# Turning attention weights by one transfer of strided squares, and tile 5 with them

## The chip, the cores and the metric

The kernel runs on one core of one Trainium2 chip. The core has five engines with queues of their own: TensorE (PE; its weight loads are shown apart as PEld), VectorE (DVE), ScalarE (ACT), GpSimd (POOL) and SyncE (SP), which in this kernel issues every transfer. The metric is the device time in microseconds. Profiled times are of one execution.

## The reference, cut to what matters

One layer of a hybrid encoder, for a prompt of 1024 positions and a sample of 32. Model width 1024; eight heads of A and eight of B, 64 wide each.

```python
def band_attention(q, k, v, q_pos, k_pos, bias_table):          # A
    s = jnp.einsum('bqhd,bkhd->bhqk', q, k).astype(jnp.float32) * ATTN_SCALE
    s = s + bias_table[:, rel].astype(jnp.float32)[None]
    s = jnp.where(ok[None, None], s, NEG_INF)                   # own chunk of 64 and the 8 before
    w = jax.nn.softmax(s, axis=-1).astype(v.dtype)
    return jnp.einsum('bhqk,bkhd->bqhd', w, v)

def stick_breaking(q, k, v, q_pos, k_pos):                      # B
    z = jnp.einsum('bqhd,bkhd->bhqk', q, k).astype(jnp.float32) * ATTN_SCALE
    causal = (k_pos[None, :] < q_pos[:, None])[None, None]
    log_1m = jnp.where(causal, jax.nn.log_sigmoid(-z), 0.0)
    after = lax.cumsum(log_1m, axis=3, reverse=True) - log_1m
    w = jnp.where(causal, jnp.exp(jax.nn.log_sigmoid(z) + after), 0.0).astype(v.dtype)
    return jnp.einsum('bhqk,bkhd->bqhd', w, v)
```

Before them stands an input projection of the normalised rows to q, k, v and a gate for A and for B; after them the gated output projection, a norm, and a second gate. Keys and values are outputs too. All is in float32.

## The kernel before

**Stages.** The rows are normalised and turned (0 to about 45 us), then the eight pairs of heads are worked off in the order A0, B0, A1, B1, A2, B2, A3, B3. While the attention of one pair runs, the q, k and v projections of the next pair are woven in as dense work for TensorE (`weave`, from L1311); beside the last pair the gate projections take their place. The output and gate products come at the end, from about 600 us.

**Precision.** A float32 product is made of two or three passes over operands split into a rounded high part and the rest. A tile that TensorE is to read is therefore written twice, by a cast on ScalarE to the high part and by a subtraction on VectorE for the low part (in attention: `wTh` and `wTl`).

**One head.** `attention` (from L834) works on the 1024 queries as eight query tiles of 128. `scores(i)` makes tile i: TensorE the products S in PSUM; in A VectorE adds the bias and finds the minimum and ScalarE takes the exponential; in B ScalarE takes the sigmoid, VectorE runs a scan and GpSimd subtracts neighbours. The weights then stand in `w1` (ring `be`), with queries on the partitions; `w0` (ring `om`) holds what came before. Tile i has `cost(i)` blocks of 128 keys: 1, 2, 3, 4, 5, 5, 5, 5 in A, and 1 to 8 in B.

`weights_t(i)` turns the weights, so that keys stand on the partitions, and has two ways:

- By TensorE: one transpose for each block into PSUM (`ptw`), four blocks to a bank, and from each bank a cast and a subtraction.
- By a round trip, for the tiles named in `ROUND` (4 and 6 before the change). VectorE transposes the 32 x 32 squares of `w1` into `w0`; SyncE writes `w0` to DRAM (`swap`); four transfers, one for each quarter of 32 partitions, bring the squares back into `w1`; then one cast and one subtraction over all columns.

`values(g)` is the product with v for tiles 0 to 3 (g = 0) and 4 to 7 (g = 1), and needs all their turned weights.

**The values' own round trip.** `values_out` (from L728) turns the projected v of a pair (128 x 1024) in the same way, with `vx` as the tile in between and back into `st`.

**Order.** The program is recorded first, and the planner (`plan`, L418, and `due`, L393) then simulates the engines with a cost for each operation (`cost`, L340) and lays down one fixed order for each of them. TensorE prefers attention to dense work. Tiles are turned two units after their scores (`LAG_T`, L32), so tile 5 is turned after the scores of tile 7. The rings `om` and `be` (L559) hand out room in turn: a new tile waits until the users of what lay there are done. A transfer waits at the head of SyncE's queue, and what is behind it waits too.

Of the kernel before, what the change touches and what calls it, by code (L numbers as in the profile page):

```python
# [13 lines left out]
P = 128  # L14
D = 1024
SEQ = 1024
# [11 lines left out]

ROUND = {"A": ((4,),(6,)), "B": ((4,),(6,))}
LAG_T = 2  # L32
LAG_V = 2
SPACE_S = 0.1
# [8 lines left out]
def f(ap):  # L43

    return ap.bitcast(F32)
# [454 lines left out]
def stream_step(  # L500
# [7 lines left out]
    nc = rec  # L508
    dma = nc.sync.dma_start
# [7 lines left out]
    def psum(tag, name):  # L517
        return ps.tile([P, 512], F32, tag=tag, name=name, bufs=PS_BUFS[tag])

    def scratch(shape, name):  # L520
        return Buf(shape, F32, name=name, real=dram.tile(shape, F32, tag=name, name=name))
# [3 lines left out]
    og_dr = scratch([8, P, T], "og_dr")  # L525
    h1_dr = scratch([T, D], "h1_dr")
    sum_dr = {w: scratch([4, 4, P, 512], f"sum_dr{w}") for w in "og"}
    r_dr = scratch([8, 768], "r_dr")
    vs_dr = {ab: scratch([NS, 512], f"vs_dr{ab}") for ab in "AB"}
    ple_dr = scratch([T, D], "ple_dr")  # L530

# [83 lines left out]
    def load_x(t):  # L615
        n = min(P, T - t * P)
        if t == 3:
            x34.append(at.tile([P, ringh.cols], F32, tag="wTh", name="x34")[:, 0:2 * D].rearrange("p (a c) -> p a c", a=2))
        xt = x34[0][:, t - 3] if t in (3, 4) else ring0.tile([P, D], f"x{t}")
        dma(xt[0:n], x_prompt[0, t * P:t * P + n, :] if t < 8 else x_sample[0])  # L620
# [8 lines left out]
    def scale_x(t, xt, n, gp):  # L629
        sq = ring1.tile([P, D], f"sq{t}")  # L630
        ms = small.tile([P, 1], F32, tag="ms", name=f"ms{t}", bufs=4)
        nc.scalar.activation(sq[0:n], xt[0:n], AF.Square, scale=1.0 / 32.0, accum_out=ms[0:n])
        r = rstd_of(ms, f"rs{t}", n)
        for kh in range(2):
            nc.vector.scalar_tensor_tensor(sq[0:n, HALF[kh]], xt[0:n, HALF[kh]], r[0:n], gp[kh][0:n], ALU.mult, ALU.mult)
        return sq
# [68 lines left out]
    def short_block(src, out, nm):  # L705
        pt = psum("T", nm)
        nc.tensor.transpose(pt[0:NS, 0:P], src[:, SEQ:T], ident)
        nc.scalar.copy(out[0:NS, 8, :], pt[0:NS, 0:P])
# [19 lines left out]
    def values_out(ab, p, src, o_p, o_s, then):  # L728

        h2 = slice(2 * p, 2 * p + 2)  # L730
        b0 = 4 if ab == "A" else 0
        box = {}

        def turn():
            st = src()
            D = scratch([P, SEQ], f"swap{ab}{p}")
            x = at2.tile([P, SEQ], F32, tag="tok", name=f"vx{ab}{p}", bufs=2)
            nc.vector.transpose(x.rearrange("p (c b f) -> p b c f", c=4, f=32), st[:, 0:SEQ])
            dma(D, x)
            for c in range(4):  # L740
                part = D[:, c * 256:(c + 1) * 256].rearrange("(g t) x -> t g x", t=32)
                dma(st[32 * c:32 * c + 32, 0:SEQ].rearrange("t (g x) -> t g x", g=4), part)
            out = at2.tile([P, NT, P], F32, tag="tok", name=f"vt{ab}{p}", bufs=2)
            box["out"] = out
            short_block(st, out, f"ptv{ab}{p}")

        def back():
            out = box["out"]
            nc.scalar.copy(out[:, 0:8, :].rearrange("p b (g f) -> p g b f", g=4), src()[:, 0:SEQ].rearrange("p (g b f) -> p g b f", g=4, f=32))
            dma(o_p[0, 0, :, h2, :].rearrange("(b p) h d -> p b (h d)", p=P), out[:, b0:8, :])  # L750
            dma(o_s[0, 0, :, h2, :].rearrange("p h d -> p (h d)"), out[0:NS, 8, :])
            then(out)

        return [(0.1, turn), (0.0, back)]
# [79 lines left out]
    def attention(ab, p, h):  # L834

        nm = f"{ab}{p}{h}"
# [12 lines left out]
        def lo_block(i):  # L849
            return max(0, i - 4) if ab == "A" else 0  # L850

        together = {i: g for g in ROUND[ab] for i in g}
        whole, done_with = {}, []

        def cost(i):
            return i + 1 - lo_block(i)
# [63 lines left out]
        def weights_t(i):  # L920
            g = i // 4
            step, size = LAID[ab, g]
            if g not in wT:
                wT[g] = [x.tile([P, size * P], f"{x.name}{nm}_{g}") for x in (ringh, ringl)]
            b0 = lo_block(i)
            w0, w1 = state.pop(i)
            n = i + 1 - b0
            at_ = ((i - 4 * g) * step + b0) * P
            hi, lo = (x[:, at_:at_ + n * P] for x in wT[g])
            if i in together:  # L930

                group = together[i]
                done_with.append((i, hi, lo))
                if i != group[-1]:
                    return
                w0, w1 = whole[group]
                m = sum(cost(x) for x in group)
                first = {x: sum(cost(y) for y in group[:k]) for k, x in enumerate(group)}
                squares = w0[:, 0:m * P].rearrange("p (c b q) -> p b c q", c=4, q=32)
                for x, _, _ in done_with:  # L940
                    y = slice(first[x], first[x] + cost(x))
                    nc.vector.transpose(squares[:, y], w1[:, y.start * P:y.stop * P])
                dr = scratch([P, m * P], f"swap{nm}_{i}")
                dma(dr, w0[:, 0:m * P])
                for c in range(4):
                    x = dr[:, c * m * 32:(c + 1) * m * 32].rearrange("(g k) x -> k g x", k=32)
                    dma(w1[32 * c:32 * c + 32].rearrange("k (g x) -> k g x", g=4), x)
                turned = w1.rearrange("p (g b q) -> p g b q", g=4, q=32)
                for x, hi, lo in done_with:
                    src = turned[:, :, first[x]:first[x] + cost(x), :]  # L950
                    hi, lo = (y.rearrange("p (b g q) -> p g b q", g=4, q=32) for y in (hi, lo))
                    nc.scalar.copy(hi, src)
                    nc.vector.tensor_tensor(lo, src, f(hi), ALU.subtract)
                done_with.clear()
                return
            for b in range(0, n, 4):
                m = min(4, n - b)
                pt = psum("T", f"ptw{nm}_{i}_{b}")
                for x in range(m):
                    nc.tensor.transpose(pt[:, x * P:(x + 1) * P], w1[:, (b + x) * P:(b + x + 1) * P], ident)  # L960
                c = slice(b * P, (b + m) * P)
                nc.scalar.copy(hi[:, c], pt[:, 0:m * P])
                nc.vector.tensor_tensor(lo[:, c], pt[:, 0:m * P], f(hi[:, c]), ALU.subtract)
# [26 lines left out]
        for i in range(8):  # L990
            out["S", i] = (0.107 * cost(i) + SPACE_S, lambda i=i: scores(i))
            out["T", i] = (0.107 * cost(i) + SPACE_T, lambda i=i: weights_t(i))
# [255 lines left out]
    for n in range(-1, 8):  # L1248
        a = len(order)
        if n < 7:  # L1250
            ab, p = pairs[n + 1]
# [458 lines left out]
    def short_product(nm, left, q):  # L1710
        o1, o2, both, minus = left
        acc = psum("S", f"{nm}8_{q}")[0:2 * NS]
        todo = ((o1, "B11"), (o2, "B21")) if q == 0 else ((both, "B22"), (minus, "T3"))
        i = 0
        for a, key in todo:
            for kt in range(KT):
                for part in range(2):
                    nc.tensor.matmul(acc, a[:, kt, :], blocks[nm, key][:, part, kt, :], start=(i == 0), stop=(i == 4 * KT - 1))
                    i += 1
        y = at2.tile([P, 512], F32, tag="bias", name=f"{nm}j8_{q}", bufs=2)  # L1720
        nc.scalar.copy(y[0:NS], acc[NS:2 * NS])
        nc.vector.tensor_tensor(y[0:NS], acc[0:NS], y[0:NS], ALU.add)
        return y[0:NS]
# [31 lines left out]
    for m, (nm, src, group) in enumerate(sets):  # L1755
        last_set = m == len(sets) - 1
        state = [{}, {}]
        for n, prod in enumerate(ORDER):
            for pair, t in enumerate(group):
                st = state[pair]  # L1760
# [28 lines left out]
                b = blocks[nm, WHICH[prod]]  # L1789
# [70 lines left out]
        if m in (0, 2):  # L1860
            if m == 0:
                row = Row(8, fb.tile([P, D], F32, tag="GP", name="h1_8"))
                row.load()
                for q in range(2):
                    y = short_product(nm, short, q)
# [3 lines left out]
            else:  # L1869
                for q in range(2):  # L1870
                    g8 = Gate(8, HALF[q])
                    y = short_product(nm, short, q)
# [38 lines left out]
```

## Time and profile before

| what | value |
|---|---|
| median of 3 runs | 799.42 us (797.0, 802.35, 799.42) |
| the profiled execution | 796.26 us |
| its span, first to last instruction | 794.2 us |
| granted TensorE clock, mean | 0.999 |

The page also shows in 40 slices of the span (19.9 us each) how busy the engines are, in tenths, and the DMA engines' mean busy share:

```profile
PE   9999989999999999999999999999999999999997
PEld 7999989999999999999999999999997877888786
DVE  6716868887688889877878788883354878676655
ACT  5636765767686548874677586532348967875741
POOL 5624546874547675424670436787544358597613
...
DMA  8519987668887759744544776756489847668634
```

A 9 is 90% or more. A matmul's end is modelled and overlaps the next one's start, so a busy share of PE says that it has work, not that it runs at its peak. A line with `xN | busy, mean ns | idle` is a group of N instructions: the time in which at least one of them ran, the mean of one, and how long the engine stood idle just before them, with what ended that. All instructions carry the line of one helper, L494, so they are told apart by their tiles.

### The profile page before, as it was taken

Reading aid. Unit: us, or ns where it says so; the run is one execution under the profiler, and the core shown is the slowest. Engines: PE = TensorE matmul, PEld = TensorE weight load, DVE = VectorE, ACT = ScalarE, POOL = GpSimd, SP = SyncE. Lnnn points to the kernel's source line nnn. Section 1 sums busy time; section 2 is a strip of 40 time slices with the busy share of each in tenths; the row PEclk is TensorE's granted clock in tenths of the full one; section 3 lists DMA queues with packets and bytes.
Section 4 is the critical chain, followed back from the end, with each engine's and each line's share of the span. In section 5 each row is a group of like instructions: output and inputs, shape, how many; then the busy total and the mean of one; then the engine's idle time right before and its main releaser. Section 6 shows DMA issues by size and latency. Waiting matters only on the chain.

```text
span 794.2 us, 14262 instructions
## 1 busy us (share of the span) xinstructions
PE 781.9 (98%) x4646; PEld 723.1 (91%) x4646; DVE 572.6 (72%) x1007; ACT 503.8 (63%) x1061; POOL 438.9 (55%) x503
## 2 busy tenths in 40 slices
PE   9999989999999999999999999999999999999997
PEld 7999989999999999999999999999997877888786
DVE  6716868887688889877878788883354878676655
ACT  5636765767686548874677586532348967875741
POOL 5624546874547675424670436787544358597613
PEclk9999999999999999999999999999999999999999
DMA  8519987668887759744544776756489847668634
GB/s 264 170 42 289 229 246 206 180 183 234 233 256 225 206 164 280 194 135 159 132 118 148 169 208 189 234 177 190 126 269 332 282 138 267 225 222 301 232 126 133
DMA packets 160971, 161.08 MB, mean 203 GB/s; under 512 B 39153, under 2 KB 120793, under 8 KB 160898
## 3 DMA queue, kind: packets, MB, share of 16 engines
q1 hardware_dynamic: 160898, 160.18, 67.4%
q8 instruction: 37, 0.61, 0.3%
q14 instruction: 36, 0.29, 0.1%
HBM read 99.23 MB, written 52.49 MB: 191 GB/s over the span
## 4 chain that ended last, share of the span: by engine, by line
PE 91%; DMA 2%; DVE 2%; POOL 2%; issue 1%; ACT 1%; SPq 1%; DVEq 0%; ACTq 0%; POOLq 0%
PE mm_gB L494 6%; PE mm_gA L494 6%; PE mm_qB L494 6%; PE mm_kB L494 6%; PE mm_vA L494 5%; PE mm_kA L494 5%; PE mm_vB L494 5%; PE mm_qA L494 5%; PE PVB L494 4%; PE SB L494 4%; PE SA L494 4%; PE PVA L494 4%; PE ptwB L494 3%; PE g0P L494 2%; PE g1P L494 2%; PE o1P L494 2%
## 5 line engine op out<-in xcount | busy, mean ns | idle before, releaser
L494 POOL TENSOR_TENSOR be<-om 128x384 f32<-128x384 f32 (+7 forms) x64 | 79.0, 1241 | 64.7 <-DVE om L494 38.8
L494 DVE TENSOR_TENSOR_SCAN om<-om,SB 128x384 f32<-128x384 f32 (+5 forms) x96 | 94.2, 999 | 8.7 <-ACT om L494 7.6
L494 ACT ACTIVATE om<-SB 128x384 f32<-128x384 f32 (+5 forms) x96 | 44.4, 492 | 34.0 <-DVE SB L494 23.0
L494 ACT ACTIVATE be<-om,statA 128x640 f32<-128x640 f32 (+4 forms) x64 | 44.5, 696 | 10.1 <-DVE statA L494 6.5
L494 ACT CAST wTh<-ptwB 128x512 fp32r<-128x512 f32 (+3 forms) x64 | 29.4, 481 | 19.5 <-PE ptwB L494 12.2
L494 DVE TENSOR_TENSOR wTl<-ptwB,wTh 128x512 fp32r<-128x512 f32 (+3 forms) x64 | 34.0, 547 | 10.4 <-ACT wTh L494 7.4
L494 DVE TENSOR_TENSOR wTl<-be,wTh 128x640 fp32r<-128x640 f32 (+1 forms) x32 | 35.3, 1105 | 4.7 <-ACT wTh L494 4.3
L494 DVE TENSOR_TENSOR wTl<-ptwA,wTh 128x512 fp32r<-128x512 f32 (+2 forms) x64 | 30.3, 483 | 10.3 <-ACT wTh L494 9.0
L494 DVE CUSTOM_DVE_ANT_0 om<-SA,biasA 128x320 f32<-128x320 f32 (+2 forms) x64 | 29.7, 483 | 9.0 <-PE SA L494 8.3
L494 ACT CAST wTh<-ptwA 128x512 fp32r<-128x512 f32 (+2 forms) x64 | 26.1, 424 | 13.3 <-PE ptwA L494 11.5
L494 DVE STREAM_TRANSPOSE om<-be 128x640 f32<-128x640 f32 (+1 forms) x32 | 29.0, 906 | 6.1 <-POOL be L494 3.5
L494 PE MATMUL SB<-klB,LB 128*128 128x384 f32 (+5 forms) x96 | 33.0, 348 | 0.0
L494 PE MATMUL SB<-kdB,LB 128*128 128x384 f32 (+5 forms) x96 | 32.9, 347 | 0.1
L494 POOL TENSOR_TENSOR oB<-oB,oB 128x256 f32<-128x256 f32 x32 | 24.2, 777 | 13.8 <-DMA oB<-in_w_out_dram 12.5
L494 DVE TENSOR_TENSOR SB<-SB,maskb 128x128 f32<-128x128 f32 x64 | 17.7, 292 | 19.1 <-PE SB L494 19.0
L494 PE MATMUL SA<-klA,LA 128*128 128x320 f32 (+2 forms) x96 | 29.4, 319 | 1.1 <-DMA klA<-klA 1.1
L494 PE MATMUL SA<-kdA,LA 128*128 128x320 f32 (+2 forms) x96 | 30.0, 323 | 0.0
L494 POOL TENSOR_TENSOR gB<-gB,gB 128x256 f32<-128x256 f32 x32 | 26.0, 832 | 6.8 <-DMA gB<-in_w_ple_gate_dram 6.7
L494 PE MATMUL ptwA<-ident,be 128*128 128x128 f32 x160 | 26.2, 273 | 2.7 <-ACT sumrowA L494 2.7
L494 ACT CAST wTh<-be 128x640 fp32r<-128x640 f32 (+1 forms) x32 | 25.0, 781 | 6.1 <-DMA be<-swapA 4.1
L494 PE MATMUL ptwB<-ident,be 128*128 128x128 f32 x192 | 28.7, 273 | 0.0
L494 POOL TENSOR_TENSOR sggA<-sggA,oggA 128x352 f32<-128x352 f32 x24 | 24.9, 1038 | 5.2 <-DMA be<-swapB 2.9
(707 smaller groups left out, 2655.0 us busy)
## 6 DMA issues: line engine op xcount, KB each, us to landing
swapA<-om SPq DMA_DIRECT2D x16, 320.0 KB, 3.6
be<-swapA SPq DMA_DIRECT2D x64, 80.0 KB, 2.8
oB<-in_w_out_dram SPq DMA_DIRECT2D x16, 256.0 KB
sum_dro<-oB SPq DMA_DIRECT2D x16, 256.0 KB, 4.3
gB<-in_w_ple_gate_dram SPq DMA_DIRECT2D x16, 256.0 KB, 4.2
sum_drg<-gB SPq DMA_DIRECT2D x16, 256.0 KB, 2.6
x<-in_x_prompt_dram SPq DMA_DIRECT2D x16, 256.0 KB, 4.1
h_dr<-h SPq DMA_DIRECT2D x8, 512.0 KB, 4.2
```

The costliest lines, as they stand in the source:

```text
L494: getattr(getattr(tc.nc, o.what[0]), o.what[1])(*args, **kw)
```

## The change

Tile 5 joins tiles 4 and 6 of every head on the round trip, as a group of its own. And the round trip's layout is another, for the weights and for the values: before, a VectorE transpose took 32 neighbouring columns for a square; now it takes every fourth column of a block of 128. The DRAM buffer gets a leading dimension of 4 (the quarter of partitions that the queries came from), and the key that row belongs to can be written as one running index, so a single transfer over all 128 partitions brings the squares back in place of four over 32. The write stays one transfer with one unbroken run for each partition, and the runs that are read back keep their length.

```diff
-ROUND = {"A": ((4,),(6,)), "B": ((4,),(6,))}
+ROUND = {"A": ((4,),(5,),(6,)), "B": ((4,),(5,),(6,))}
...
         def turn():
             st = src()
-            D = scratch([P, SEQ], f"swap{ab}{p}")
+            D = scratch([4, P, SEQ // 4], f"swap{ab}{p}")
             x = at2.tile([P, SEQ], F32, tag="tok", name=f"vx{ab}{p}", bufs=2)
-            nc.vector.transpose(x.rearrange("p (c b f) -> p b c f", c=4, f=32), st[:, 0:SEQ])
-            dma(D, x)
-            for c in range(4):
-                part = D[:, c * 256:(c + 1) * 256].rearrange("(g t) x -> t g x", t=32)
-                dma(st[32 * c:32 * c + 32, 0:SEQ].rearrange("t (g x) -> t g x", g=4), part)
+            nc.vector.transpose(x.rearrange("p (c b f) -> p b c f", c=4, f=32), st[:, 0:SEQ].rearrange("p (b t c) -> p b c t", c=4, t=32))
+            dma(D.rearrange("g (t c) x -> (g t) (c x)", c=4), x)
+            dma(st[:, 0:SEQ].rearrange("p (g x) -> p g x", g=4), D.rearrange("g p x -> p g x"))
...
                 for x, _, _ in done_with:
                     y = slice(first[x], first[x] + cost(x))
-                    nc.vector.transpose(squares[:, y], w1[:, y.start * P:y.stop * P])
-                dr = scratch([P, m * P], f"swap{nm}_{i}")
-                dma(dr, w0[:, 0:m * P])
-                for c in range(4):
-                    x = dr[:, c * m * 32:(c + 1) * m * 32].rearrange("(g k) x -> k g x", k=32)
-                    dma(w1[32 * c:32 * c + 32].rearrange("k (g x) -> k g x", g=4), x)
+                    nc.vector.transpose(squares[:, y], w1[:, y.start * P:y.stop * P].rearrange("p (b k c) -> p b c k", c=4, k=32))
+                dr = scratch([4, P, m * 32], f"swap{nm}_{i}")
+                dma(dr.rearrange("g (k c) x -> (g k) (c x)", c=4), w0[:, 0:m * P])
+                dma(w1.rearrange("p (g x) -> p g x", g=4), dr.rearrange("g p x -> p g x"))
```

Counted over the kernel: 88 PE transposes go (5 for each of 8 heads of A, 6 for each of 8 of B), 16 VectorE transposes and 16 round trips come, and a round trip is two transfers in place of five.

## The prediction

> **What bounds the kernel now.** I read the page first (the engines' busy shares, the chain that ended last, the DMA share), then TensorE's own waits.
>
> ```profile
> span 794.2 us, 14262 instructions
> ...
> PE 781.9 (98%) x4646; PEld 723.1 (91%) x4646; DVE 572.6 (72%) x1007; ACT 503.8 (63%) x1061; POOL 438.9 (55%) x503
> ...
> q1 hardware_dynamic: 160898, 160.18, 67.4%
> ...
> PE 91%; DMA 2%; DVE 2%; POOL 2%; issue 1%; ACT 1%; SPq 1%; DVEq 0%; ACTq 0%; POOLq 0%
> ```
>
> TensorE (PE) is busy for 98% of the span and makes 91% of the chain that ended last. Work taken from PE shortens the kernel, as long as nothing new makes PE wait. In TensorE's list of waits, those inside the attention stage are few:
>
> ```profile
> PE ptwA L494 <- ACT sumrowA L494: 2.7, 1, 2.7
> ...
> PE SA L494 <- DMA klA<-klA: 1.1, 1, 1.1
> ```
>
> Together they are 3.8 us. The dense projections fill PE whenever attention is not ready. The change touches attention alone, which runs from about 66 to 570 us. I cut it into the eight head pairs, A and B by turns, by the times at which their last outputs leave. The columns after the length are the busy us of PE, of its weight loads, of VectorE (DVE), ScalarE and GpSimd, each with its instruction count; then the granted clock, the DMA share and GB/s.
>
> ```profile
> 66.00:112.00 46.00, 42.18 (x278) 40.63 (x276) 33.88 (x80) 33.05 (x73) 20.38 (x26) 1.00 0.95 273
> 112.00:180.00 68.00, 67.92 (x430) 65.64 (x429) 56.47 (x85) 43.17 (x88) 48.13 (x54) 1.00 0.67 192
> 180.00:240.00 60.00, 60.00 (x397) 58.18 (x397) 43.17 (x104) 45.38 (x100) 28.76 (x44) 1.00 0.83 234
> 240.00:308.00 68.00, 67.37 (x436) 64.85 (x436) 58.76 (x94) 40.95 (x92) 51.67 (x61) 1.00 0.73 218
> 308.00:346.00 38.00, 38.00 (x250) 36.64 (x249) 30.27 (x72) 31.04 (x71) 13.70 (x18) 1.00 0.82 218
> 346.00:418.00 72.00, 72.00 (x460) 70.11 (x459) 58.75 (x92) 46.11 (x93) 38.60 (x39) 1.00 0.44 124
> 418.00:472.00 54.00, 54.00 (x363) 52.57 (x363) 41.85 (x101) 39.94 (x93) 14.10 (x22) 1.00 0.66 176
> 472.00:570.00 98.00, 98.00 (x626) 96.00 (x624) 67.89 (x102) 44.18 (x96) 67.54 (x70) 1.00 0.63 189
> sum 504.00, PE 499.47 PEld 484.62 DVE 391.05 ACT 323.81 POOL 282.88; mean PE 62.43 PEld 60.58 DVE 48.88 ACT 40.48 POOL 35.36
> ```
>
> PE fills every pair but the first. VectorE comes second: 391 of 504 us, 78%, and in the second B pair 58.76 of 68, or 86%. The granted clock is 1.00 throughout, so it isn't a term. DMA is nearly full in the first A pair alone (0.95).
>
> **What leaves TensorE.** Tile 5 of a head has 5 key blocks in A and 6 in B, one PE transpose each, for 8 heads of each kind: 88 of the 160 + 192. The 273 ns of one overlap its neighbours, so I take what a run of transposes costs from the timeline, as the time from its start to the start of what follows.
>
> ```profile
> L494 PE MATMUL ptwB<-ident,be 128*128 128x128 f32 x192 | 28.7, 273 | 0.0
> L494 PE MATMUL ptwA<-ident,be 128*128 128x128 f32 x160 | 26.2, 273 | 2.7 <-ACT sumrowA L494 2.7
> ```
> ```profile
> 75.27 0.71 PE L494 MATMUL ptwA<-ident,be 128*128 128x128 f32 x5
> 75.73 0.57 PE L494 MATMUL mm_kB<-hnl,wh_kB 128*128 128x352 f32 x2
> ...
> 163.18 0.82 PE L494 MATMUL ptwB<-ident,be 128*128 128x128 f32 x6
> 163.75 0.57 PE L494 MATMUL mm_qA<-hnl,wh_qA 128*128 128x352 f32 x2
> ```
>
> Five cost 0.46 us and six 0.57 us. So 8 x 0.46 + 8 x 0.57 = 8.2 us leave PE, all on the path.
>
> **What VectorE and ScalarE get.** The groups by shape:
>
> ```profile
> L494 DVE TENSOR_TENSOR_SCAN om<-om,SB 128x512 f32<-128x512 f32 x24 | 30.3, 1262 | 0.8 <-ACT om L494 0.5 <-POOL ksS L494 0.2
> L494 DVE TENSOR_TENSOR wTl<-be,wTh 128x640 fp32r<-128x640 f32 x24 | 24.3, 1012 | 4.5 <-ACT wTh L494 4.1
> L494 DVE TENSOR_TENSOR_SCAN om<-om,SB 128x384 f32<-128x384 f32 x24 | 23.9, 994 | 1.3 <-ACT om L494 1.2
> L494 DVE TENSOR_TENSOR wTl<-ptwB,wTh 128x512 fp32r<-128x512 f32 x32 | 21.5, 679 | 7.4 <-ACT wTh L494 4.7 <-PE PVB L494 2.6
> L494 DVE STREAM_TRANSPOSE om<-be 128x640 f32<-128x640 f32 x24 | 20.1, 839 | 6.1 <-POOL be L494 3.5 <-ACT be L494 2.2
> L494 DVE TENSOR_TENSOR wTl<-ptwA,wTh 128x512 fp32r<-128x512 f32 x24 | 16.5, 688 | 6.9 <-ACT wTh L494 6.6
> L494 DVE TENSOR_TENSOR wTl<-be,wTh 128x896 fp32r<-128x896 f32 x8 | 11.1, 1383 | 0.2 <-ACT wTh L494 0.2
> L494 DVE STREAM_TRANSPOSE om<-be 128x896 f32<-128x896 f32 x8 | 8.8, 1105 | 0.1
> L494 DVE TENSOR_TENSOR wTl<-ptwB,wTh 128x256 fp32r<-128x256 f32 x16 | 6.6, 413 | 1.1 <-ACT wTh L494 1.1
> L494 DVE TENSOR_TENSOR wTl<-ptwA,wTh 128x128 fp32r<-128x128 f32 x24 | 6.6, 280 | 1.3 <-ACT wTh L494 1.3
> L494 DVE STREAM_TRANSPOSE ktA<-stkA 128x512 f32<-128x512 f32 x4 | 2.8, 703 | 11.4 <-ACT stkA L494 11.4
> ```
>
> An A head gives up two evictions from PSUM (688 + 280 ns) and gets a 640 transpose (839) and a 640 subtraction in SBUF (1012): 0.88 us more. A B head gives up 679 + 413 and gets 768 columns of each; between the rows for 640 and 896 that is about 972 + 1198: 1.08 us more. Eight of each make 15.7 us on VectorE. At 391 of 504 us it has room for this beside PE, so it costs nothing; what it costs without that room is a rival below. ScalarE casts the same columns from another place, two calls becoming one, and is at 324 of 504: nothing.
>
> All 56 transposes then also read every fourth column. No row shows a strided read. The transposes for 512, 640 and 896 columns lie on one line of 1.05 ns a column, though the first writes densely and the others in runs of 32. The slowest VectorE op by the column is the scan, (1262 - 994) / 128 = 2.1 ns. So the stride costs between 0 and 1.05 ns a column; a gain I exclude, since a broken-up write pattern already changes nothing. The columns are 8 x 1920 in A, 8 x 2304 in B and 8 x 1024 for the values, 41,984 in all: 0 to 44 us of VectorE time. I take the low end, since the nearest rows are transposes of the same operation at one pace whatever the pattern; the high end is the first rival.
>
> **What the queue and the transfers get.** Quoted: the issues of the returns and of a weight load (min, median and max ns); then, around TensorE's longest attention wait, SyncE's queue in the timeline and two pieces of the chain.
>
> ```profile
> L494 SPq DMA_DIRECT2D be<-swapA x64: 302/432/866, 84.0 to 467.6; - x64
> ...
> L494 SPq DMA_DIRECT2D wr_kA<-in_w_in_dram x8: 383/612/1670, 6.9 to 310.1; - x8
> ```
> ```profile
> 108.06 3.93 SPq L494 DMA_DIRECT2D be<-swapA  x8
> ```
> ```profile
> 104.41 2.85 DMA swapA<-om
> ...
> 111.56 2.61 DMA be<-swapA
> ```
>
> A round trip's four returns take about 4 x 432 = 1728 ns to issue. One return of 512 runs (128 partitions, 4 each) is nearest to the weight loads, also 128 x 4: 612 ns. So the 40 existing round trips each give back 1.1 us of the queue, 45 us in all, and the 16 new ones take 16 x (432 + 612), about 17 us. From 108.06 us on, the issue of eight returns, 3.93 us, lies on the chain between the landing of the write and that of the returns, so some shortening is possible; the bound is the 3.8 us of waits above. I take none.
>
> Each new trip also adds a wait: SyncE's queue stands until the write has landed (2.85 us in the chain) before it can issue the return, and behind it stand weight loads and attention outputs. That is how the 2.7 us wait came about: the output's transfer was issued behind that landing, ScalarE's sum row waited for it, and PE for the row. Of the 40 trips now, one did this; 16 more at that rate cost 16/40 x 2.7 = 1.1 us. The values of tile 5 themselves aren't urgent: tile 7 is worked off after them, ahead of the product.
>
> The new trips move 8 x 2 x 320 KB and 8 x 2 x 384 KB (128 partitions of 640 or 768 columns of 4 bytes, out and back), 11.5 MB. At 67.4% of 794 us for 160 MB that is 3.3 us a MB, 38 us of DMA time over 504 us, 7 points. Only the first pair is short of room: 1.3 MB, 4.4 us, bring its 0.95 over 1 by some 2 us. Bounds 0 and 2 us; I take 1.0.
>
> **The sum.** -8.2 + 1.1 + 1.0 = -6.1 us. The profiled execution took 796.26 us (span 794.2), so it would take 790.2; it is 3.2 us below the median of the runs shown, 799.42. On that median I forecast 793. Alone, this case reaches from 787 (all of -8.2 and the 3.8 us of waits gone) to 798 (the new waits three times as dear).
>
> **Rivals.** *The strided read runs at half pace and VectorE becomes the bound.* For it: VectorE has little room in the B pairs. An A pair gets 2 x (0.88 + 2.0) + 1.07 = 6.8 us, a B pair 2 x (1.08 + 2.4) + 1.07 = 8.0. The second B pair would have 66.8 of 68 us, the third A pair 37.1 of 38. If VectorE can't run denser than the 86.4% it has shown, six of the eight pairs stretch, by 1.1, 6.7, 0, 9.3, 4.9, 5.3, 2.3 and 0 us: 29.6 us. If it can run at 100%, none does. Half of it, 14.8, gives 799.4 - 6.1 + 14.8 = 808; the ends are 793 and 823. It decides from 6.1 us of stretch on. Against it: equal pace of the transposes so far.
>
> [...]
>
> *The queue's new waits eat the gain.* If 3 of the 16 new trips, not 16/40 of one, stall PE for 2.7 us as the one above, 8.1 us are gone: 799. For it: the queue is in order, and a tile's two buffers stay taken for the whole trip, two landings of 2.85 and 2.61 us at least, so the next head's scores may wait for room. Against: TensorE hardly waits for the 40 trips there are, and returns get shorter.
>
> **Chances.** Forecast 0.44, half-pace rival 0.41, queue rival 0.15. Within 1% (8 us) is about what a measurement of this kernel can tell from no change. 793 lies at the edge of it, so I split 0.44 into 0.28 faster and 0.16 same; the half-pace case into 0.02, 0.12 and 0.27 slower; the queue's into 0.09 same and 0.06 slower. That is 0.30 faster, 0.37 same, 0.33 slower. Cases of both signs count, so the range runs from 787 to 816, leaving out the half-pace case's top.
>
> **What would show it.** Right: PE transposes fall from 352 to 264; PE's busy time falls by about 8 us in attention and its list of waits hardly grows; the 640 transpose stays near 839 ns. The half-pace rival: that row reads about 1.5 us, VectorE is above 90% in the B pairs, and TensorE's waits name VectorE. The queue rival: the transposes keep their price, but PE waits on ScalarE or on transfers behind a landing. The forecast is wrong if PE's busy time falls and the span does not.

## The result and the profile after

The median of 20 runs of the changed kernel is 801.33 us (798.72 to 805.98), beside 799.8 us for 20 runs of the kernel before on the same chip. The ratio is 1.0032, with a 95% interval from 1.0017 to 1.0046. By the ratio the kernel became about 2.5 us slower, by the two medians 1.5. That is a loss of a third of a per cent, clear of the noise, where the forecast of 793 us was a gain of 0.8%.

The profiled execution of the changed kernel took 805.19 us, 3.9 us more than its own median. Two others took 801.06 and 801.51 us. The one of the kernel before, at 796.26, is 3.5 below its median. So the two profiles lie 8.9 us apart, and what follows shows the loss larger than it is.

From its page: the span, the engines' busy time (share of the span, instructions), the transfer queue (packets, MB, share) and the shares of the chain that ended last.

```profile
span 803.4 us, 13859 instructions
...
PE 780.4 (97%) x4558; PEld 712.8 (89%) x4558; DVE 622.3 (77%) x1007; ACT 500.3 (62%) x1043; POOL 436.9 (54%) x503
...
q1 hardware_dynamic: 169730, 171.70, 70.0%
...
PE 68%; DVE 13%; DMA 6%; issue 5%; ACT 4%; POOL 3%; SPq 1%; DVEq 0%; POOLq 0%; ACTq 0%
```

TensorE (PE) has 88 matmuls fewer (4646 to 4558), as the diff says, but its busy time fell by only 1.5 us; it also holds time in which matmuls followed each other more slowly than usual, as the count of gaps below shows. The chain tells more: PE makes 68% of it where it made 91%, and VectorE (DVE) 13% where it made 2%. The end is now set by PE and others by turns. (A faster order of the same kernel, with the constant 56 below, has 72% and 11%, so these shares don't tell a slow order from a fast one.)

The VectorE groups, changed kernel (count, then busy us and mean ns of one, then the idle time ahead of them):

```profile
L494 DVE STREAM_TRANSPOSE om<-be 128x640 f32<-128x640 f32 x32 | 42.4, 1335 | 1.1 <-ACT be L494 0.9 <-POOL om L494 0.2
L494 DVE STREAM_TRANSPOSE om<-be 128x896 f32<-128x896 f32 x8 | 14.5, 1809 | 0.5 <-POOL be L494 0.4
L494 DVE STREAM_TRANSPOSE om<-be 128x768 f32<-128x768 f32 x8 | 12.5, 1561 | 0.0
L494 DVE STREAM_TRANSPOSE vxA<-stvA 128x1024 f32<-128x1024 f32 x4 | 8.2, 2055 | 1.0 <-ACT stvA L494 1.0
L494 DVE STREAM_TRANSPOSE ktB<-stkB 128x1024 f32<-128x1024 f32 x4 | 5.0, 1240 | 0.1
```

A transpose of 640 columns takes 1335 ns where it took 839. From 640 to 896 columns it gains (1809 - 1335) / 256 = 1.85 ns a column, where the dense ones have 1.05. The last row is a control in the same kernel: `kt` is still transposed from neighbouring columns, and its 1024 columns take 1240 ns, against 2055 for the 1024 strided columns of `vx`. So the stride costs 0.80 ns a column, about 34 us of VectorE over the 41,984 columns. With the 15.7 us for tile 5 that makes 49.3 us. The page has 622.3 - 572.6 = 49.7.

The attention stage by pairs of heads, cut as before at the last output of a pair (length; busy us and instruction count of PE, its loads, VectorE, ScalarE, GpSimd; granted clock, DMA share, GB/s):

```profile
66.00:112.00 46.00, 44.92 (x289) 42.97 (x288) 38.25 (x87) 36.37 (x78) 20.01 (x28) 1.00 0.99 293
112.00:180.00 68.00, 65.92 (x410) 63.20 (x410) 61.84 (x82) 40.98 (x81) 49.37 (x55) 1.00 0.76 224
180.00:240.00 60.00, 56.92 (x365) 54.73 (x364) 51.60 (x102) 40.18 (x95) 27.27 (x40) 0.97 0.85 252
240.00:308.00 68.00, 67.14 (x421) 63.49 (x421) 62.59 (x82) 39.98 (x84) 48.70 (x60) 1.00 0.73 226
...
356.00:426.00 70.00, 67.78 (x418) 63.74 (x417) 66.75 (x86) 43.36 (x87) 36.19 (x36) 1.00 0.57 160
...
sum 516.00, PE 501.71 PEld 478.40 DVE 439.46 ACT 321.90 POOL 283.13; mean PE 62.71 PEld 59.80 DVE 54.93 ACT 40.24 POOL 35.39
```

Before, PE had no work in 504.00 - 499.47 = 4.5 us of this stage, and 46.00 - 42.18 = 3.8 of these fell in the first pair. Now it has none in 516.00 - 501.71 = 14.3 us, spread over all pairs. TensorE's waits (us in all, times, the longest) say for whom:

```profile
PE SsA L494 <- DVE QsA L494: 2.5, 1, 2.5
PE SA L494 <- DVE statA L494: 1.9, 3, 1.0
PE ptwB L494 <- issue: 1.8, 2, 1.2
PE SB L494 <- DVE om L494: 1.4, 3, 0.6
...
PE ptsA L494 <- DVE wTl L494: 1.1, 1, 1.1
PE ptwB L494 <- POOL QfsB L494: 1.0, 1, 1.0
```

Four of the six name VectorE. In the first three B pairs VectorE is busy for 61.84 of 68 us (91%), 62.59 of 68 (92%) and 66.75 of 70 (95%). By the signs that the prediction wrote down, this is the half-pace rival: a dear transpose, VectorE over 90% in the B pairs, waits that name it. The experiments show that these signs aren't enough.

Busy time hides what a stall costs, so one more count helps: for each matmul the time from its start to the next one's start. The median for its shape, summed over all matmuls, is PE's usual time; what is over that is gaps. Some 6.4 us of each span lie ahead of the first matmul and behind the last start. In us:

```
                      usual   gaps    span
before                770.5   17.3   794.2
after                 761.4   35.5   803.4
```

PE's own work shrank by 9.1 us, and its gaps grew by 18.2. The difference, 9.1, is the span's (9.2). So the work did leave PE, and in these two executions twice as much came back as waiting. By the ratio of the two kernels, a loss of 2.5 us, it was about 9.1 + 2.5 = 11.6 us. The question is what brought the gaps.

### The profile page after: what moved, and what is told of

Its sections match the earlier page's. It is cut to its first block, busy times and chain, and to the rows that moved or that the text cites. A ratio compares the mean times of both kernels' runs of the same rounds, so it can differ in the third digit from the quotient of the medians.

```text
span 803.4 us, 13859 instructions
## 1 busy us (share of the span) xinstructions
PE 780.4 (97%) x4558; PEld 712.8 (89%) x4558; DVE 622.3 (77%) x1007; ACT 500.3 (62%) x1043; POOL 436.9 (54%) x503
## 3 DMA queue, kind: packets, MB, share of 16 engines
q1 hardware_dynamic: 169730, 171.70, 70.0%
## 4 chain that ended last, share of the span: by engine, by line
PE 68%; DVE 13%; DMA 6%; issue 5%; ACT 4%; POOL 3%; SPq 1%; DVEq 0%; POOLq 0%; ACTq 0%
PE mm_gB L494 6%; DVE om L494 5%; PE mm_qA L494 5%; PE mm_gA L494 4%; PE mm_kA L494 4%; PE PVB L494 4%; PE SB L494 3%; DMA be<-swapA 3%; PE mm_qB L494 3%; PE mm_vB L494 3%; PE g0P L494 2%; PE g1P L494 2%; PE o1P L494 2%; PE g2P L494 2%; PE o0P L494 2%
## 5 line engine op out<-in xcount | busy, mean ns | idle before, releaser
L494 POOL TENSOR_TENSOR be<-om 128x896 f32<-128x896 f32 (+7 forms) x64 | 76.3, 1200 | 73.0 <-DVE om L494 28.6
L494 DVE STREAM_TRANSPOSE om<-be 128x640 f32<-128x640 f32 (+2 forms) x48 | 69.3, 1451 | 1.6 <-ACT be L494 0.9
L494 DVE TENSOR_TENSOR wTl<-be,wTh 128x640 fp32r<-128x640 f32 (+2 forms) x48 | 54.5, 1142 | 16.7 <-ACT wTh L494 16.6
L494 ACT CAST wTh<-be 128x640 fp32r<-128x640 f32 (+2 forms) x48 | 37.5, 781 | 24.0 <-DMA be<-swapB 14.4
L494 ACT CAST wTh<-ptwB 128x512 fp32r<-128x512 f32 (+3 forms) x48 | 22.3, 479 | 16.9 <-PE ptwB L494 12.4
L494 PE MATMUL SA<-klA,LA 128*128 128x320 f32 (+2 forms) x96 | 29.6, 319 | 0.8 <-DMA klA<-klA 0.8
L494 DVE TENSOR_TENSOR wTl<-ptwB,wTh 128x512 fp32r<-128x512 f32 (+3 forms) x48 | 25.2, 538 | 3.6 <-PE PVB L494 2.6
L494 ACT CAST wTh<-ptwA 128x128 fp32r<-128x128 f32 (+3 forms) x48 | 19.6, 423 | 11.9 <-PE ptwA L494 11.7
L494 POOL TENSOR_TENSOR klB<-stkB,kdB 64x1024 fp32r<-64x1024 f32 x8 | 19.1, 2392 | 14.4 <-ACT kdB L494 11.4
L494 DVE TENSOR_TENSOR wTl<-ptwA,wTh 128x128 fp32r<-128x128 f32 (+3 forms) x48 | 22.6, 478 | 3.8 <-ACT wTh L494 3.4
L494 POOL TENSOR_TENSOR h<-h,x 128x512 f32<-128x512 f32 (+1 forms) x18 | 23.8, 1353 | 0.0
```

Source lines behind the costliest of these rows:

```text
L494: getattr(getattr(tc.nc, o.what[0]), o.what[1])(*args, **kw)
```

## The experiments

Four theories stand against each other. **Load**: the strided read fills VectorE, which then holds PE up. **Trip**: the longer way of tile 5 (write, landing, return) holds its buffers and SyncE's queue. **Price**: the planner charges a transpose 100 + 1.04 ns a column whatever its stride, and lays down an order that VectorE can't keep. **Order**: any edit makes the planner lay down another order, and one order differs from another by as much as the change is worth. The last came in with the second batch of runs. The recorded expectations have other names for some: load is their stride theory, price is the order theory of the first batch, and order is their lottery and later their draw theory.

**One part at a time.** The layout alone: the changed kernel with tiles 4 and 6 on the round trip.

```diff
-ROUND = {"A": ((4,),(5,),(6,)), "B": ((4,),(5,),(6,))}
+ROUND = {"A": ((4,),(6,)), "B": ((4,),(6,))}
```

> The new layout alone: squares of every fourth column and one return, but tiles 4 and 6 only, so PE keeps all 352 transposes. Stride theory (the strided read costs VectorE 1.85 in place of 1.05 ns a column, and PE then waits for VectorE): the 640 transpose reads about 1335 ns, 30,720 strided columns make 25 us more on VectorE, and nothing is saved on PE, so the time is 3 to 8 us above before (ratio 1.004 to 1.010), with PE waits that name VectorE. Trip theory (what costs is tile 5's own round trip, by queue waits and ring room): nothing of that is here and the queue has 120 issues less, so the ratio is 1.000 or a little under it.

Measured: 800.43 us, ratio 1.0015 [1.0001, 1.0028], under the 1.004 to 1.010 of the load theory. The groups show the full price of the stride:

```profile
L494 DVE STREAM_TRANSPOSE om<-be 128x640 f32<-128x640 f32 x24 | 32.1, 1339 | 4.8 <-POOL be L494 2.7 <-POOL om L494 1.2 <-ACT be L494 0.7
```

Tile 5 alone: the kernel before, dense squares and four returns, with tile 5 on the round trip.

```diff
-ROUND = {"A": ((4,),(6,)), "B": ((4,),(6,))}
+ROUND = {"A": ((4,),(5,),(6,)), "B": ((4,),(5,),(6,))}
```

> Tile 5 alone: the round trip for tiles 4, 5 and 6, in the old layout (dense squares, four returns). Stride theory: the 640 transpose stays at 839 ns, 8.2 us of PE work go and VectorE has 16 us more, which it has room for: 5 to 8 us faster than before (ratio 0.990 to 0.994). Trip theory: slower than before, ratio 1.003 or above, since the 16 new waits of the queue are here, with five issues each.

Measured: 807.66 us, ratio 1.0108 [1.0083, 1.0133], where the load theory had 0.990 to 0.994, with transposes at their old pace:

```profile
L494 DVE STREAM_TRANSPOSE om<-be 128x640 f32<-128x640 f32 x32 | 26.6, 832 | 5.5 <-POOL be L494 2.9 <-ACT be L494 2.4
```

PE's usual time is 761.2 us, 9.3 below before, and its gaps are 39.2. So the part without any stride loses most. The parts don't add up either: 0.15% and 1.08% alone, 0.32% together. This spoke for the trip theory.

The stride with four returns of 32 partitions and no tile 5, so that the issue time saved by the single return is taken back:

```diff
-                dma(w1.rearrange("p (g x) -> p g x", g=4), dr.rearrange("g p x -> p g x"))
+                for c in range(4):
+                    r = slice(32 * c, 32 * c + 32)
+                    dma(w1[r].rearrange("p (g x) -> p g x", g=4), dr[:, r].rearrange("g p x -> p g x"))
```

(the values' return likewise, and `ROUND` as in the layout alone)

> Tiles 4 and 6 with squares of every fourth column, but brought back by four returns of 32 partitions as before. Beside the layout alone it tells the strided read from the one return. Stride theory: equal to the layout alone within 0.3%, and slower than before by 3 to 8 us. Return theory (one return of 320 KB and more lands later, 4.4 to 7.0 us against 2.8 to 3.3, and that is what PE waits for): ratio to before 1.000 within 0.2%, below the layout alone.

Measured: 801.09 us, 1.0026 [1.0007, 1.0044]. Beside the 1.0015 of the layout alone the intervals overlap: the single return isn't seen to be worth anything, each in one order.

**The planner told of the stride.** The changed kernel, with its work untouched and the planner's price for strided transposes set to the measured one:

```diff
+            if method == "transpose" and len(reads[0].shape) > 2:
+                return 150 + 1.85 * n, 85
```

> The changed kernel with one line more: the planner is told that a strided transpose takes 150 + 1.85 ns a column in place of 100 + 1.04, so that the order laid down fits what the chip does. Order theory (PE waits because the fixed order expects VectorE earlier than it comes): at least half of the 18 us of added gaps between matmuls goes, ratio to before 0.985 to 0.995. Load theory (VectorE is simply too full in the B pairs, 62 of 68 us): ratio within 0.3% of the changed kernel's 1.003, the waits only in other places.

Measured: 792.21 us, 0.9919 [0.9895, 0.9943], faster than both. Its page:

```profile
span 793.3 us, 13868 instructions
...
PE 776.2 (98%) x4558; PEld 714.5 (90%) x4558; DVE 618.0 (78%) x1007; ACT 505.8 (64%) x1047; POOL 439.0 (55%) x503
```

VectorE is as loaded as in the changed kernel (618.0 us against 622.3), each strided transpose is as dear, and the gaps are 25.8 us instead of 35.5. So a VectorE with this load doesn't have to hold PE up. That fits the price theory, and the next batch tried to break it.

**The wrong price given to the kernel before.** Its dense turning transposes, unchanged, are charged as if they were strided:

```diff
+            if method == "transpose" and writes[0].buf.name[0:2] != "kt":
+                return 150 + 1.85 * n, 85
```

> The control for the order: the kernel before, every instruction and shape as it was, but the planner is told 150 + 1.85 ns a column for its dense turning transposes, which really take 1.05. Price theory (the time follows how well the told price fits, and too low a price is what hurts, since PE then comes before VectorE is done): too high a price only leaves slack, ratio to before 0.998 to 1.003. Lottery theory (any other order lands somewhere within a per cent either way, and the known price was a lucky draw): the ratio lies anywhere, with more than 0.5% either way as likely as not.

Measured: 809.09 us, 1.012 [1.0082, 1.0158], with the same operations on the same data, where the price theory had 0.998 to 1.003. This is the largest loss of the study, and all that differs is the order.

**Half of the price**, in the changed kernel (the line above with 125 + 1.45 ns):

> The changed kernel, with the planner told half of the strided transposes' extra price: 125 + 1.45 ns a column. Price theory: between the changed kernel (1.003) and the one with the price known (0.992), so 0.994 to 1.001. Lottery theory: no such order among the three; outside of that band as likely as not.

Measured: 802.18 us, 1.0024 [1.0004, 1.0044], nothing gained over the changed kernel's 1.0032.

**The right price for the layout alone** (150 + 1.85 ns, tiles 4 and 6):

> The layout alone (tiles 4 and 6, fourth columns, one return) with the price known, 150 + 1.85 ns. Price theory: it falls from 1.0015 to 0.997 to 1.000, so that the layout costs nothing once the order fits, and tile 5 is worth 4 to 7 us of the 8.2 beside it (0.992 against this one). If instead the price matters only where VectorE is nearly full, as with tile 5, this one stays at 1.0015 within 0.15%.

Measured: 803.75 us, 1.0049 [1.0026, 1.0072]. Here the true price made nothing faster: 1.0015 became 1.0049, with intervals that just touch. The price theory, by which a truer price should give a better order, fails in both.

**Every other column.** The changed kernel with squares of every second column, a step of 8 bytes for 16, and two returns of 64 partitions:

```diff
-                dr = scratch([4, P, m * 32], f"swap{nm}_{i}")
-                dma(dr.rearrange("g (k c) x -> (g k) (c x)", c=4), w0[:, 0:m * P])
-                dma(w1.rearrange("p (g x) -> p g x", g=4), dr.rearrange("g p x -> p g x"))
+                dr = scratch([2, 4, P // 2, m * 32], f"swap{nm}_{i}")
+                dma(dr.rearrange("h g (k c) x -> (g k) h (c x)", c=2), w0[:, 0:m * P].rearrange("p (h y) -> p h y", h=2))
+                for e in range(2):
+                    dma(w1[64 * e:64 * e + 64].rearrange("p (g x) -> p g x", g=4), dr[e].rearrange("g p x -> p g x"))
```

(the transposes' patterns and the values' trip accordingly; the planner's price stays at 100 + 1.04 ns a column)

Two things are asked: the pace of the 640 transpose, which takes 1335 ns at every fourth column and 839 dense, and the time of the kernel.

> [...] For the time, if the transposes are back: price theory 0.989 to 0.994, since the old price fits again and PE has 8.2 us less; trip theory (tile 5's extra trips stall PE by themselves, as in tile 5 alone at 1.011): 1.003 or above.

Measured: 806.38 us, 1.0075 [1.0049, 1.01]. Its groups:

```profile
L494 DVE STREAM_TRANSPOSE om<-be 128x640 f32<-128x640 f32 x32 | 26.3, 828 | 3.1 <-ACT be L494 2.8
L494 DVE STREAM_TRANSPOSE om<-be 128x896 f32<-128x896 f32 x8 | 8.8, 1095 | 0.2 <-POOL be L494 0.2
...
L494 DVE STREAM_TRANSPOSE vxA<-stvA 128x1024 f32<-128x1024 f32 x4 | 4.9, 1222 | 0.6 <-ACT stvA L494 0.6
```

At a step of two columns the transposes run at the dense pace, 828 ns for 640 columns beside 839. VectorE is relieved of the whole cost of the stride (582.1 us busy), and the kernel is slower than with it. As what decides the sign, the load theory falls here: neither is the load enough (the planner told of the stride), nor is it needed (this one, and tile 5 alone).

This run bears the sign of the prediction's queue rival instead. TensorE waits most for ScalarE's casts of turned weights:

```profile
PE PVA L494 <- ACT wTh L494: 5.9, 6, 1.6
PE PVB L494 <- ACT wTh L494: 4.4, 2, 2.8
```

ScalarE for its part stood idle for 30 us ahead of these casts until returns had landed, beside 22 in the changed kernel. The issues of the round trips hold SyncE's queue for 105 us here and 141 in tile 5 alone, where the changed kernel has 55. So the two dense kernels with tile 5 differ from it in the queue too.

**Other orders of the same work.** What all these kernels had in common, the gains and the losses, was only that the planner had been given something else to work from. So the planner's constant for a semaphore between engines, which is used for nothing else, was moved by 2 or 4 ns in both kernels:

```diff
-SEM = 60
+SEM = 58
```

(and 56, 62 and 64)

> The kernel before with one planner constant moved from 60 to 58 ns (the time it reckons for a semaphore); work and shapes are the same, the order laid down is another. Draw theory (every order is a draw, and the order before is a good one of them, so that any edit draws again): slower than before, ratio 1.002 to 1.012. Price theory (the order only matters through prices that are far off): 2 ns change nothing, ratio 0.998 to 1.002.

> The same with 62 ns: a second draw. Draw theory: 1.002 to 1.012, by chance above or below the one with 58. Price theory: 0.998 to 1.002.

> A third draw of the order before (56 ns for a semaphore, work and shapes the same). Draw theory: 1.002 to 1.012, above the order before as the two others (1.0076 and 1.0047).

> A fourth draw of the order before (64 ns). Draw theory: 1.002 to 1.012.

> The changed kernel with 58 ns: a draw of the changed kernel's orders. Draw theory: anywhere from 0.992 to 1.010 of before; it is the mean over the draws that tells what the change itself is worth. If its 8.2 us on PE are real, the mean of the changed kernel's draws lies below the mean of the draws of before; if the strided reads eat them, the two means agree within 0.3%. Price theory: as the changed kernel, 1.001 to 1.005.

> The changed kernel with 62 ns: another draw; expected as for 58. Draw theory: 0.992 to 1.010 of before. Price theory: 1.001 to 1.005.

> A fourth draw of the changed kernel (56 ns), beside 1.0032, 0.9973 and 1.0011. If the 8.2 us on PE are kept for the most part, its draws have a mean 5 to 8 us (0.6 to 1.0%) below the mean of the redrawn kernel before, here 0.994 to 1.004; if the strided reads eat them, it lies with the draws of before, 1.004 to 1.012.

> A fifth draw of the changed kernel (64 ns); expected as for 56: 0.994 to 1.004 if the work taken from PE is kept, 1.004 to 1.012 if it is eaten.

Measured, as ratios to the kernel before:

| constant | kernel before | changed kernel |
|---|---|---|
| 60 | 1 | 1.0032 [1.0017, 1.0046] |
| 56 | 1.0054 [1.0028, 1.0081] | 0.9929 [0.9901, 0.9957] |
| 58 | 1.0076 [1.0031, 1.0121] | 0.9973 [0.995, 0.9995] |
| 62 | 1.0047 [1.002, 1.0074] | 1.0011 [0.9983, 1.0038] |
| 64 | 1.0004 [0.9977, 1.003] | 1.0048 [1.0024, 1.0072] |
| mean of five | 1.0036 | 0.9999 |

The orders do differ. With equal neighbours among TensorE's matmuls put in one row, the traces of the kernel before have 1818 rows at 60 and 1815 at 58, and it takes 595 rows out or in to make one of the other.

The changed kernel runs from 0.9929 to 1.0048 by order alone, 1.2%, with intervals that are far apart. The order that the kernel before happens to have is the best of its five, though the one at 64 isn't told apart from it. That one, at 1.0004, misses the 1.002 to 1.012 that the draw theory had for it; the changed kernel at 56 and 64 came out just beyond the two ends of the 0.994 to 1.004 for work that is kept. Two views of the changed kernel with constant 56, the span and the attention stage by pairs, show how little the load decides:

```profile
span 790.3 us, 13864 instructions
```
```profile
112.00:180.00 68.00, 66.45 (x414) 64.11 (x413) 61.66 (x77) 38.56 (x78) 51.04 (x54) 1.00 0.73 227
...
237.00:301.00 64.00, 62.50 (x396) 59.32 (x395) 58.13 (x82) 38.79 (x84) 44.49 (x55) 1.00 0.76 229
...
349.00:417.00 68.00, 67.25 (x420) 64.61 (x420) 64.36 (x87) 42.55 (x83) 37.30 (x37) 1.00 0.58 168
...
sum 503.00, PE 496.11 PEld 476.25 DVE 433.83 ACT 324.85 POOL 285.26; mean PE 62.01 PEld 59.53 DVE 54.23 ACT 40.61 POOL 35.66
```

VectorE is at 91%, 91% and 95% in the first three B pairs, as dense as in the changed kernel at 60, with the same operations. Yet PE lacks work in 503.00 - 496.11 = 6.9 us of the stage and not 14.3, and the span is 13 us shorter.

**The known price in other orders.** If the right price itself made a good order, it would do so with other constants too:

> The changed kernel with the price known (150 + 1.85 ns a column) and 58 ns for a semaphore: a second order with the right price. If the right price is a gain by itself, 0.989 to 0.995, near the first one's 0.992. If that one was a lucky order, this lies among the changed kernel's draws, 0.993 to 1.005, with a mean of 0.999.

> The same with 62 ns, a third order with the right price: 0.989 to 0.995 if the price is a gain by itself, 0.993 to 1.005 around 0.999 if it was luck.

Measured: 1.0002 [0.9976, 1.0028] and 0.9996 [0.9973, 1.0019]. With 0.9919 the three orders have a mean of 0.9972, against 1.0005 for the changed kernel at 58, 60 and 62. Most of the 0.9919 was a good order, then, and not the worth of a true price; three orders a side can't exclude a worth of 0.3%.

What is the change worth, order aside? The means of five orders differ by 0.38 points, 3.0 us, in favour of the changed kernel. Taken as independent draws (standard deviations 0.33 and 0.48 points) the 95% interval reaches from 0.98 points faster to 0.22 slower, or from -7.8 to +1.8 us. It holds the forecast's -6.1 us, and zero. Without the two orders at 60 the means are 1.0045 and 0.9990, 4.4 us apart, a little less than the 5 to 8 us expected if the work taken from PE is kept for the most part.

**Which part brings the gaps.** The count of usual time and gaps, made for all kernels with one and the same usual time for each shape of matmul (so the figures differ a little from those above), says which part. PE's usual time is 770.4 us without tile 5 and 760.9 with it, 9.5 less. The gaps, of one profiled execution each, in us:

| kernels | gaps |
|---|---|
| before, constants 60, 56, 58, 62, 64 | 17.3, 27.8, 24.8, 23.4, 21.7 |
| stride without tile 5 (layout alone, four returns, price known) | 21.4, 22.4, 26.3 |
| before, wrong price | 37.2 |
| changed kernel, constants 60, 56, 58, 62, 64 | 35.9, 22.8, 27.8, 28.4, 34.0 |
| changed kernel, other prices (known, half, known at 58 and 62) | 25.8, 29.6, 31.3, 30.9 |
| tile 5 without the stride of four (tile 5 alone, every other column) | 39.3, 37.3 |

The stride alone leaves the gaps as they are: a mean of 23.4 us beside 23.0. With tile 5 on the round trip the mean over the nine kernels with the stride is 29.6, and the two without it have more. An order alone can do as much, as the wrong price shows. Between the five orders of each kernel the gaps grow by 6.8 us, with an interval from 0 to 13. So the best estimate is that some 7 of the 9.5 us that tile 5 takes from PE come back as waiting, and that this comes with tile 5, not with the stride. These sums were made after all the runs, and no experiment was planned for them. What about tile 5 does it isn't told apart: the trips, VectorE's 15.7 us more, or only that PE has less work to fill its waits with.

## Why the prediction was wrong

**What leaves TensorE: right.** 352 transposes became 264. Predicted were 8.2 us of PE's time; the usual time shrank by 9.1.

**VectorE's work: tile 5 about right, stride mis-sized.** The 15.7 us for tile 5 and the stride's 33.6 make 49.3, where the page shows 49.7; tile 5 alone adds 13.2 in its own run (585.8 us busy). "I take the low end" of 0 to 1.05 ns a column was wrong: it is 0.80. The rows it was argued from differ only in how they write, so they said nothing of a read in which neighbours lie 16 bytes apart. The rival was right that this read is slow: 640 columns take 1335 ns at a step of 16 bytes, 828 at a step of 8, and 839 dense. No run shows why the one step costs and the other doesn't. The loss is a factor of 1.76 by the column (1.85 against 1.05 ns) and 1.6 for the 640 columns, not the 2 of "half pace", the high end of the author's estimate.

**"It has room for this beside PE, so it costs nothing": not refuted for the stride, open for tile 5.** With 434 us of VectorE in 503 us the changed kernel at constant 56 has 0.9929. The rival's sum of 14.8 us for six stretched pairs doesn't follow from its mechanism: in that order VectorE is busy for 91 to 95% of the first three B pairs, and PE's gaps are 22.8 us, beside 23.0 on average in the orders of before.

**The queue: right that it gets shorter.** The changed kernel's issues of the returns, min, median and max ns:

```profile
L494 SPq DMA_DIRECT2D be<-swapA x24: 370/484/1169, 84.4 to 478.1; - x24
```

A return of 512 runs takes 484 ns to issue, not the 612 of the weight loads. All trips together hold the queue for 55 us, where they held it for 91 (issues summed over the trace). From the write's issue to the cast it takes 11.5 us on average, as before. Nothing of this is seen in the end, going by the layout with one return and with four: "I take none" held. As for the second rival, TensorE's waits in the changed kernel hardly name a transfer or ScalarE behind one (0.8 us for `kl`, 0.7 for a cast of turned weights); its sign is plainest at every other column, where the queue is held for longer. The chain's share of DMA did rise, from 2% to 6%, so the trips play some part in this order. The 11.5 MB more are there (160.18 to 171.70), and the first pair's DMA share went from 0.95 to 0.99; what that cost can't be told apart.

**The step that failed: the sum took PE's waits as those of before plus two small terms.** 1.1 us for the queue's new waits and 1.0 for the DMA share stood for all that PE would wait more; "its list of waits hardly grows". Its gaps grew by 18.2 us in the profiled execution. By the table of gaps above, about 7 of these come with tile 5 on the mean of five orders; some 6 are there because the order of before has fewer gaps than the mean of its five, and some 6 because this order of the changed kernel has more than the mean of its own. For these 12 there was no term at all. Behind that stands an assumption that the prediction never wrote down: that the order around the change stays. The planner lays the whole program anew, and the order of before, the best of five, wasn't kept by any of the edits. Against the mean of its four redraws, 1.0045, it has 0.45% (3.6 us) to lose, and the changed kernel's spread of 1.2% comes on top. A sum of 6.1 us, 0.8%, is no larger than that. The stated range, 787 to 816, did hold the result, by luck: for a reason that wasn't in it.

**What is shown and what isn't.** Shown: the price of the stride, the 9 us that left PE, that the same operations in another order give 793 to 803 us, and that neither VectorE's load nor the price in the planner decides the sign. Estimated from sums made afterwards: that gaps grow with tile 5 and not with the stride. Not shown: the worth of the change itself, whose interval takes in zero; what in tile 5's trip makes the gaps; whether dense squares with tile 5 (1.0108, and 1.0075 at every other column) are worse for a reason or are two poor orders, since each was run in one order only; and whether the stride costs a few us that better orders hide. A write spread over several transfers, with a dense read, wasn't tried.

Two versions beat both kernels by 0.7% or more: the changed kernel with the planner told of the stride, 792.21 us, and with the constant at 56, 793.05 us. The second does it by its order alone, the first mostly so.

## What to carry to other kernels

Where a planner or scheduler lays down the whole order, an edit is compared with one draw, and the draw before may be a good one: redraw both sides by moving a constant that changes no work before an effect below 1% is put down to the edit or argued from a busy share. Five orders a side told here only what is larger than 0.6%. Signs that a theory predicts (an engine above 90%, waits that name it) can all be there and still not be the cause; look for a kernel with the same signs and another time. When a VectorE transpose of float32 reads with a stride, price the stride first: every second column cost nothing here (828 ns for 640 columns, 839 dense), every fourth 0.8 ns a column.

## What the runs showed that was not expected

**A subtraction stretched more than sixfold.** The longest TensorE wait of the changed kernel stands behind a subtraction of 256 columns of `Qs`. In its timeline (start, us, engine, operation, count):

```profile
202.18 4.75 POOL L494 TENSOR_TENSOR gB<-gB,gB 128x256 f32<-128x256 f32 x6
...
203.53 3.68 DVE L494 TENSOR_TENSOR QsA<-QfsA,QsA 128x256 fp32r<-128x256 f32 x1
...
207.26 0.82 PE L494 MATMUL SsA<-Kh0sA,QsA 128*128 128x272 f32 x2 [2.51 <-DVE QsA L494]
```

The kernel before has the same operation at 568 ns on average:

```profile
L494 DVE TENSOR_TENSOR QsA<-QfsA,QsA 128x256 fp32r<-128x256 f32 x2 | 1.1, 568 | 1.7 <-ACT QsA L494 1.7
```

It takes 3.68 us while GpSimd runs one operation on two operands after another beside it, and ends 0.3 us after they do. It isn't the only one. Of the changed kernel's 32 subtractions of 640 turned columns, which have both operands in SBUF, the 12 with no GpSimd operation beside them take 793 to 825 ns, the 20 others 800 to 2675. Those of 512 columns with one operand in PSUM take 644 to 693 ns with GpSimd beside them (24) or without (16). Tile 5 goes over from the second kind to the first. Which operations meet is a matter of the order too, so this may be one way in which an order gets its price. That GpSimd holds VectorE off wasn't tried by itself.

**After a wait of 2.5 us the granted clock was 0.50.** Windows of the changed kernel before, just after and later than this wait (columns as above; the granted clock is the third number from the right):

```profile
200.00:204.00 4.00, 4.00 (x28) 4.00 (x27) 3.07 (x2) 2.19 (x4) 4.00 (x3) 1.00 1.00 271
207.20:211.00 3.80, 3.73 (x17) 3.74 (x18) 2.40 (x8) 1.54 (x4) 0.00 (x0) 0.58 0.93 216
211.00:214.00 3.00, 3.00 (x20) 2.75 (x19) 1.96 (x6) 1.60 (x5) 0.72 (x1) 1.00 0.91 234
```

The granted clock is 0.58 on average over the 3.8 us after the wait, by the trace 0.50 from 207.00 to 210.41 us. A pair of `SsA` matmuls of one shape takes some 0.45 us to the next start there (207.88 to 208.34, 208.34 to 208.79 us) and 0.25 ahead of the wait (202.97 to 203.22, 203.22 to 203.47). At 0.42 x 3.8 that is an estimated 1.6 us more. The waits list doesn't show it, since PE counts as busy. In tile 5 alone, the 6 us from 329 us on, with the end of a wait of 2.08 us in them, have a clock of 0.72. That the wait lowers the clock wasn't tried by itself. The lowered clock is part of the profiled execution's loss, whose mean clock was 0.996; the executions of 801.06 and 801.51 us had 0.999 and 1.000.
